# When the projections of the next heads must be finished: at the head boundary, or one unit ahead of it

## Chip, cores and metric

One NeuronCore of one Trainium2 chip runs the whole kernel. The metric is the device time of one execution in microseconds (us). The profile shows one execution with its engines: TensorE (PE for the matmuls, PEld for its weight loads), VectorE (DVE), ScalarE (ACT), GpSimd (POOL) and SyncE (SP, which here only issues transfers).

## The reference, cut to what matters

Two layers of a transformer-like trunk work on 512 latent tokens and 256 context tokens, all 1024 wide. In each layer a normalised input `h` is projected once, and three token mixers run on the result; their outputs are gated, merged and projected, and a mixture of 16 experts follows. The two mixers that matter here are both attentions:

```
ka, va, kb, vb, qa, qb, u, v, gates = _split(h @ w_in[i], KV_SIZES + Q_SIZES)
ya = neighbourhood_attn(qa, ka, va, kac, vac, na_rpb[i])      # A: 8 heads of 64, window + context keys
s  = einsum('bqhcd,bkhcd->bhcqk', q, k) * (dh ** -0.5)        # B: 4 heads, two softmax maps each
p  = softmax(s);  a = p[:, :, 0] - lam * p[:, :, 1];  yb = a @ v
```

In layer 0 the context tokens are computed too; in layer 1 they only give keys and values. So there are six attention stages: A and B for the context in layer 0, A and B for the latents in layer 0, A and B for the latents in layer 1.

## The kernel before, in words

**Units.** A stage A works through four pairs of heads (`pr` 0 to 3), a stage B through four double heads (`hd` 0 to 3). For each pair or head it goes through blocks of 128 queries, `b` from 0 to `nb - 1`: `nb` is 4 for the latents and 2 for the context. One (pair, block) is a unit. A unit has scores (`S`, line 487, matmuls of Q against K into PSUM), a softmax on VectorE and ScalarE (`soft`), transposes of the probabilities (`T`), the product with the values (`PV`) and an output step (`post`). `pipeline` (line 489) writes the units out so that the scores of the next unit stand ahead of the transposes of this one:

```
for i, u in enumerate(units):
    nxt = units[i + 1] if i + 1 < len(units) else None
    if nxt is not None:
        pre(nxt)
        S(nxt)
    ...
    F.pump(); T(u); ...soft(nxt); F.pump(); ...post(prev); PV(u); F.pump()
```

**Filler.** So that TensorE has work while a softmax runs, every other projection of the layer stands in a queue `F` (class `Filler`, line 48) of generators, each cut into small steps of three to twenty-four matmuls. `F.pump()` emits a share of what is left: `left / pumps`, in the planner's own microseconds, with 12 x `nch` pumps planned for a stage (`nch` is the number of blocks, so three pumps per unit). `F.finish(name)` emits steps until the named item is complete, whatever the share. The planner books a projection of 128 columns of output for 512 tokens as 24 matmuls and 5.12, and one step of three matmuls as 0.64; for 256 tokens half of it.

**Queue.** For stage A `mix` (line 804) pushes the values `va`, then for `i` = 1, 2, 3 the projections of K and Q of pair `i` (`kqa i`) and two gate projections, and last K and Q for the first head of stage B. For stage B it pushes the merge of A's output, the values `vb`, then `kqb i` with two gates each, and the gMLP's v. In layer 1 K is projected for the context tokens too, so a pair costs 12.80 instead of 10.24.

**K and Q.** `g_qk` (line 410) splits a weight tile in two halves (lines 153 and 155), multiplies (line 322), splits K (lines 349, 350), and likewise Q (`split_q`, lines 358 and 359). The half of Q that has to stand on the other 64 partitions is copied by a transfer from SBUF to SBUF, issued on ScalarE's queue (line 361), one for each of the two heads of a pair. The scores need that copy.

**Before the first score of a unit** stands `pre(nxt)`, which the change touches. Weights are loaded by SP (line 147), the bias of a unit in stage A too (line 537). The order that is written is a priority: the framework's scheduler then sets the order on each engine, and an instruction that is written later can run earlier when what stands ahead of it isn't ready by the scheduler's reckoning. Side work, vector products for the modulation of later layers (line 259, with its own weight loads), is handed out at a fixed rate for each microsecond of filler.

Of the kernel before, what the change touches and what calls it, by code (L numbers as in the profile page):

```python
# [38 lines left out]
def fr(ap):  # L39
    return ap.bitcast(F32)  # L40
# [68 lines left out]
class Trunk:  # L109
# [404 lines left out]
    def neighbourhood(self, c, F):  # L514
        nc, t = self.nc, self.t
        l, n, lat = c.l, c.n, c.lat
        nb = n // P
# [5 lines left out]

        def pre(u):
            pr, b = u
            if b == 0:
                F.finish(("kqa", pr))

        def S(u):
            pr, b = u  # L530
            K, Q = c.KQ["a", pr]
            qs = slice(b * P, (b + 1) * P)
            ps = self.p2([P, 2, 512])[:, :, :W]
            bias = None
            if lat:
                bias = self.tl([P, 2, 256], F32, "w2")
                nc.sync.dma_start(bias, t["bias"][l, pr, b])
            for hh in range(2):
                if not lat:
                    self.scores(ps[:, hh, :], Q, hh, qs, K[hh])  # L540
                    continue
                if KSTART[b] is None:
                    k = K[hh][:, 0:768].rearrange("p (a c) -> p a c", c=384)[:, :, 0:128]
                else:
                    k = K[hh][:, KSTART[b]:KSTART[b] + 256]
                self.scores(ps[:, hh, 256:512], Q, hh, qs, K[hh][:, NLAT:768])
                self.scores(ps[:, hh, 0:256], Q, hh, qs, k)
            st[u] = [ps, bias]
# [57 lines left out]
        def post(u):  # L606
# [7 lines left out]
            else:  # L614
                self.split_ps(y[pr][:, 0, :], y[pr][:, 1, :], yps)

        self.pipeline(F, [(pr, b) for pr in range(4) for b in range(nb)], pre, S, soft, T, PV, post)
        return y

# [13 lines left out]
    def differential(self, c, F, y):  # L633
        nc, t = self.nc, self.t
        l, n, lat = c.l, c.n, c.lat
        nk = 768 if lat else NCTX
        nt = nk // P
        nb = n // P
        st = {}

        def pre(u):
            hd, b = u
            if b == 0:
                F.finish(("kqb", hd))

        def S(u):
            hd, b = u
            K, Q = c.KQ["b", hd]
            qs = slice(b * P, (b + 1) * P)
            pss = []  # L650
            for m in range(2):
                ps = self.p2([P, nk])
                if lat:
                    self.scores(ps[:, n:], Q, m, qs, K[m][:, n:])
                self.scores(ps[:, :n], Q, m, qs, K[m][:, :n])
                pss.append(ps)
            st[u] = pss

        def soft(u):
            pss = st[u]  # L660
            ex, sm, rc = [], [], []
            for m in range(2):
                nm = self.st()
                nc.vector.tensor_reduce(out=nm, in_=pss[m], axis=AX.X, op=ALU.max, negate=True)
                e = self.tl([P, nk], F32, "e")
                s1 = self.st()
                nc.scalar.activation(e, pss[m], AF.Exp, bias=nm, accum_out=s1)
                r1 = self.st()
                nc.vector.reciprocal(r1, s1)
                ex.append(e)  # L670
                sm.append(s1)
                rc.append(r1)
            rat = self.st()
            nc.vector.scalar_tensor_tensor(out=rat, in0=sm[0], scalar=self.neglam[:, l:l + 1], in1=rc[1],
                                           op0=ALU.mult, op1=ALU.mult)
            nc.vector.scalar_tensor_tensor(out=ex[0], in0=ex[1], scalar=rat, in1=ex[0], op0=ALU.mult, op1=ALU.add)
            st[u] = [ex[0], rc[0]]

        def T(u):
            ex, rc = st[u]  # L680
            pT = self.tl([P, nk], F32, "e")
            for g in range(0, nt, 3):
                w = min(3, nt - g)
                tps = self.p1([P, w * P])
                for j in range(w):
                    nc.tensor.transpose(tps[:, j * P:(j + 1) * P], ex[:, (g + j) * P:(g + j + 1) * P], self.ident)
                nc.scalar.copy(pT[:, g * P:(g + w) * P], tps)
            st[u] = [pT, rc]

        def PV(u):  # L690
            hd, b = u
            F.finish("vb")
            pT, rc = st[u]
            V = c.V["b"]
            ops = self.p1([P, P])
            for j in range(nt):
                nc.tensor.matmul(ops, lhsT=pT[:, j * P:(j + 1) * P], rhs=V[j][:, hd * P:(hd + 1) * P],
                                 start=(j == 0), stop=(j == nt - 1))
            on = self.tl([P, P], F32, "w2")
            ss = self.st()  # L700
            nc.scalar.activation(on, ops, AF.Square, scale=rc, accum_out=ss)
            r = self.rstd(ss, P)
            sc = self.st()
            nc.vector.tensor_mul(sc, r, rc)
            nc.vector.tensor_scalar_mul(on, ops, sc)
            st[u] = on

        def post(u):
            hd, b = u
            qs = slice(b * P, (b + 1) * P)  # L710
            F.finish("mergeA")
            if not y:
                y.extend(self.ytiles(n))
            ot = self.p1([P, P])
            nc.tensor.transpose(ot, st[u], self.ident)
            g = self.subg[:, l:l + 1]
            nc.scalar.activation(y[hd][:, 0, qs], ot, AF.Copy, scale=g)
            nc.vector.scalar_tensor_tensor(out=y[hd][:, 1, qs], in0=ot, scalar=g, in1=fr(y[hd][:, 0, qs]),
                                           op0=ALU.mult, op1=ALU.subtract)

        self.pipeline(F, [(hd, b) for hd in range(4) for b in range(nb)], pre, S, soft, T, PV, post)
        return y

# [967 lines left out]
```

## Time and profile before

| | us |
|---|---|
| median of 3 runs | 2731.29 (2729.12 to 2732.53) |
| the profiled execution's own time | 2727.76 |
| its span in the trace | 2726.0 |
| TensorE busy in the span | 2491.0 (91%) |
| VectorE, ScalarE busy | 1674.9 (61%), 1238.0 (45%) |
| TensorE idle before a score that waited for the copy of Q | 23.6, 14 times |

The span is the time from the first to the last instruction of the program in that execution. The granted clock is the share of TensorE's full clock that it was given. "Idle before" is the time in which an engine did nothing just ahead of an instruction, and the name behind the arrow is what ended that time.

### The profile page before, as it was taken

The numbers are of one execution on the slowest core, as the hardware profiler recorded it, in microseconds if no ns is written. First come the engines' busy times: TensorE is split into PE (matmuls) and PEld (weight loads), VectorE is DVE, ScalarE is ACT, GpSimd is POOL, SyncE is SP. The second block draws the span as 40 slices with busy tenths as digits, with TensorE's granted clock in tenths as the row PEclk, the third lists the DMA queues.
The fourth block names the chain that finished last, engine by engine and source line by source line (L and its number), as shares of the span: only waits on it lengthen the run. The fifth ranks groups of instructions, "written<-read, shape, count | busy, mean of one in ns | idle before, by whom it ended". The sixth has DMA issues, their size and how long they took to land.

```text
span 2726.0 us, 35390 instructions
## 1 busy us (share of the span) xinstructions
PE 2491.0 (91%) x12856; PEld 1744.1 (64%) x12856; DVE 1674.9 (61%) x2841; ACT 1238.0 (45%) x2251; POOL 220.3 (8%) x155
## 2 busy tenths in 40 slices
PE   7898989999999789999999899998999969888886
PEld 5788877777788656666666687787788833111111
DVE  7567766878696579999999855656765341100002
ACT  4456445435623378888888655534453220000000
POOL 0000000001000011122222100000000011000000
PEclk8999999999999889999999999999999979999999
DMA  7465554343247689999999353252223579999998
GB/s 278 156 229 173 204 186 128 113 143 107 84 157 258 244 284 379 372 372 371 375 374 377 111 167 118 72 163 62 85 78 118 207 301 399 402 403 403 402 403 338
DMA packets 189278, 653.81 MB, mean 240 GB/s; under 512 B 22096, under 2 KB 26576, under 8 KB 189104
## 3 DMA queue, kind: packets, MB, share of 16 engines
q1 hardware_dynamic: 175648, 612.68, 60.6%
q0 software_dynamic: 8464, 25.96, 3.7%
q10 hardware_dynamic: 4992, 12.92, 1.8%
q8 instruction: 101, 1.65, 0.2%
q14 instruction: 73, 0.60, 0.1%
HBM read 615.03 MB, written 25.95 MB: 235 GB/s over the span
## 4 chain that ended last, share of the span: by engine, by line
PE 58%; DMA 20%; DVE 14%; ACT 5%; issue 2%; POOL 1%; SPq 0%; POOLq 0%; ACTq 0%; DVEq 0%
PE p L322 23%; PE p L1241 16%; DMA h<-in_w_e 5%; PE p L462 5%; DVE w L155 4%; PE p L1072 3%; PE p L1402 3%; DMA y<-in_w_e 3%; DMA w<-in_w_e 2%; DMA q<-q 2%; PE p L487 2%; DMA raw<-in_w_e 2%; DMA e<-in_w_e 2%; PE p L602 1%; ACT w L153 1%
## 5 line engine op out<-in xcount | busy, mean ns | idle before, releaser
L322 PE MATMUL p<-h,w 128*128 128x512 f32 (+1 forms) x4416 | 915.6, 358 | 16.3 <-DVE w L155 4.5
L322 PEld LDWEIGHTS p<-h,w 128*128 128x128 f32 x4416 | 710.4, 191 | 137.5 <-issue 11.8
L155 DVE TENSOR_TENSOR w<-raw,w 128x1024 fp32r<-128x1024 f32 x289 | 351.0, 1222 | 236.5 <-ACT w L153 208.8
L153 ACT CAST w<-raw 128x1024 fp32r<-128x1024 f32 x289 | 302.7, 1052 | 390.1 <-PE p L322 164.5
L1241 PE MATMUL p<-w,k 128*96 128x512 f32 x1536 | 376.0, 400 | 12.4 <-DVE w L155 9.6
L1241 PEld LDWEIGHTS p<-w,k 128*96 128x96 f32 x1536 | 238.9, 163 | 119.8 <-DVE w L155 20.9
L155 DVE TENSOR_TENSOR w<-h,w 128x1024 fp32r<-128x1024 f32 x156 | 185.5, 1220 | 10.1 <-ACT w L153 6.7
L167 POOL TENSOR_TENSOR st<-st,mhalf 128x1 f32<-128x1 f32 x76 | 57.4, 755 | 1564.4 <-DVE st L165 1564.4
L1241 PE MATMUL p<-w,q 128*96 128x512 f32 x768 | 180.0, 393 | 0.2 <-ACT q L1255 0.2
L153 ACT CAST w<-h 128x1024 fp32r<-128x1024 f32 x156 | 161.6, 1049 | 31.4 <-PE p L1241 27.2
L462 PE MATMUL p<-y,w 128*128 128x512 f32 (+1 forms) x864 | 175.0, 358 | 0.4 <-ACT y L342 0.3
L259 DVE SCALAR_TENSOR_TENSOR w<-raw,raw 128x1024 bf16<-128x1024 f32 x128 | 155.9, 1221 | 23.6 <-DMA raw<-in_w_adaT 16.5
L462 PEld LDWEIGHTS p<-y,w 128*128 128x128 f32 x864 | 142.6, 188 | 27.5 <-ACT y L342 0.8
L1241 PEld LDWEIGHTS p<-w,q 128*96 128x96 f32 x768 | 123.8, 161 | 53.7 <-ACT q L1255 0.4
L1435 ACT COPY q<-p 128x256 f32<-128x256 f32 x32 | 10.3, 375 | 303.3 <-PE p L1415 303.3
L487 PE MATMUL p<-k,q 128*128 128x256 f32 (+1 forms) x576 | 110.0, 323 | 30.7 <-DMA q<-q 23.6
L1333 POOL DMA_INDIRECT x1a<-tg,idx x16 | 96.0, 5997 | 457.9 <-DVE w L1287 408.8
L1447 DVE TENSOR_TENSOR v<-v,p 128x512 f32<-128x512 f32 x16 | 11.0, 688 | 171.0 <-PE p L1402 159.8
L487 PEld LDWEIGHTS p<-k,q 128*128 128x128 f32 x576 | 84.3, 196 | 47.4 <-issue 15.2
L1402 PE MATMUL p<-h,k 128*64 128x512 f32 x356 | 91.8, 628 | 16.9 <-DMA h<-in_w_e 16.6
L1427 DVE TENSOR_TENSOR k<-p,modAlat 128x256 f32<-128x256 f32 x32 | 12.1, 419 | 139.4 <-PE p L1415 139.4
L1072 PE MATMUL p<-w,h 128*128 128x512 f32 x384 | 91.1, 395 | 1.1 <-DVE w L155 1.1
(336 smaller groups left out, 3196.9 us busy)
## 6 DMA issues: line engine op xcount, KB each, us to landing
h<-in_w_e SPq DMA_DIRECT2D x288, 512.0 KB, 7.4
raw<-in_w_in SPq DMA_DIRECT2D x164, 512.0 KB, 3.5
raw<-in_w_e SPq DMA_DIRECT2D x120, 512.0 KB, 8.0
e<-in_w_e SPq DMA_DIRECT2D x96, 512.0 KB, 7.2
y<-in_w_e SPq DMA_DIRECT2D x96, 512.0 KB, 7.8
m<-in_w_e SPq DMA_DIRECT2D x92, 512.0 KB, 7.8
raw<-in_w_adaT SPq DMA_DIRECT2D x80, 512.0 KB, 3.9
w<-in_w_e SPq DMA_DIRECT2D x60, 512.0 KB, 10.2
```

The costliest lines, as they stand in the source:

```text
L153: nc.scalar.copy(hi, fr(raw))
L155: nc.vector.tensor_sub(lo, fr(raw), fr(hi))
L167: nc.gpsimd.tensor_tensor(out=r, in0=v, in1=self.mhalf, op=ALU.pow)
L259: nc.vector.scalar_tensor_tensor(out=dump, in0=fr(raw), scalar=1.0, in1=self.cb[v], op0=ALU.mult, op1=ALU.mult, accum_out=self.mod[s, l][: ...
L322: nc.tensor.matmul(ps, lhsT=w[a][:, k * P:(k + 1) * P], rhs=h[k][:, b, :], start=(k == 0 and i == 0), stop=(k == KD - 1 and i == 2))
L462: nc.tensor.matmul(bps, lhsT=wb[a][:, (jj * 4 + k) * P:(jj * 4 + k + 1) * P], rhs=y[k][:, b, :], start=(k == 0 and i == 0), stop=(k == 3 a ...
L487: nc.tensor.matmul(ps, lhsT=Q[:, h, i, qs], rhs=k, start=(i == 0), stop=(i == 1))
L602: nc.tensor.matmul(ypsd[pr][64 * hh:64 * hh + 64, b * P:(b + 1) * P], lhsT=V[vi][:, head * 64:(head + 1) * 64], rhs=pT[hh][:, j * P:(j + 1 ...
L1072: nc.tensor.matmul(banks[i][hf], lhsT=c.mh[k][:, a, i * P:(i + 1) * P], rhs=w[b][:, hf * BW:(hf + 1) * BW], start=(k == 0 and p == 0), sto ...
L1241: nc.tensor.matmul(ps[:, hf * 512:(hf + 1) * 512], lhsT=xt[a][:, k, :M], rhs=w[b][:, hf * 512:(hf + 1) * 512], start=(k == 0 and i == 0), ...
L1333: nc.gpsimd.indirect_dma_start(out=dst[:, :], out_offset=bass.IndirectOffsetOnAxis(ap=self.idx[:M, e:e + 1], axis=0), in_=y, in_offset=Non ...
L1402: nc.tensor.matmul(ps[half(h), :], lhsT=xT[:, k, :], rhs=w[:, h * BW:(h + 1) * BW], start=(k == 0), stop=(k == KD - 1))
```

## The change

In both attention stages the demand for the next pair's K and Q moves. Before, it stands ahead of the first unit of that pair (`b == 0`). After, only the first pair is asked for there; the next pair is asked for ahead of the scores of the last block of the current pair (`b == nb - 1`). `finish` emits all that stands in the queue ahead of the named item as well, so `va`, `mergeA`, `vb` or gates come along when they are still in the queue. Nothing is added or taken away; only the place in the written order changes, and with it how much the later pumps have left to hand out.

```
         def pre(u):
             pr, b = u
-            if b == 0:
+            if b == 0 and pr == 0:
                 F.finish(("kqa", pr))
+            if b == nb - 1 and pr < 3:
+                F.finish(("kqa", pr + 1))
...
         def pre(u):
             hd, b = u
-            if b == 0:
+            if b == 0 and hd == 0:
                 F.finish(("kqb", hd))
+            if b == nb - 1 and hd < 3:
+                F.finish(("kqb", hd + 1))
```

## Rows read from the trace of the kernel before

**Rows 1.** The page's first lines: span; busy time, share, instructions.

```profile
span 2726.0 us, 35390 instructions
PE 2491.0 (91%) x12856; PEld 1744.1 (64%) x12856; DVE 1674.9 (61%) x2841; ACT 1238.0 (45%) x2251; POOL 220.3 (8%) x155
```

**Rows 2.** Windows, one per attention stage in order, first score to last.

```profile
core 0: us, PE busy (x) PEld busy (x) DVE busy (x) ACT busy (x) POOL busy (x), PEclk, DMA share, GB/s
52.00:141.00 89.00, 76.06 (x600) 69.61 (x600) 57.17 (x101) 44.86 (x106) 0.00 (x0) 0.96 0.55 184
141.00:220.00 79.00, 71.23 (x565) 68.60 (x564) 50.56 (x108) 44.35 (x103) 4.19 (x6) 0.96 0.63 214
346.00:495.00 149.00, 136.35 (x808) 106.66 (x809) 88.92 (x204) 77.59 (x208) 0.00 (x0) 0.98 0.44 145
495.00:730.00 235.00, 224.13 (x1183) 181.48 (x1182) 188.03 (x367) 113.41 (x244) 15.78 (x16) 0.99 0.36 118
1588.00:1752.00 164.00, 160.91 (x1020) 130.66 (x1019) 84.49 (x201) 84.08 (x232) 0.00 (x0) 1.00 0.37 118
1752.00:1996.00 244.00, 229.23 (x1266) 191.36 (x1265) 158.89 (x287) 109.65 (x237) 8.23 (x14) 0.98 0.30 95
```

**Rows 3.** One line's view: all scores (line 487), TensorE, what ended its idle time.

```profile
  DMA q<-q: 23.6, 14
```

**Rows 4.** Timeline, TensorE: waits for Q at later pairs; start, busy us, [idle before].

```profile
73.51 0.50 PE L487 MATMUL p<-k,q 128*128 128x256 f32 x2 [2.14 <-DMA q<-q]
...
175.18 0.80 PE L487 MATMUL p<-k,q 128*128 128x256 f32 x2 [2.68 <-DMA q<-q]
...
1879.80 1.62 PE L487 MATMUL p<-k,q 128*128 128x256 f32 x4 [4.38 <-DMA q<-q]
...
1926.75 0.93 PE L487 MATMUL p<-k,q 128*128 128x256 f32 x4 [1.10 <-DMA q<-q]
```

**Rows 5.** Timeline, TensorE: the three such waits at a stage's first pair.

```profile
346.59 1.22 PE L487 MATMUL p<-k,q 128*128 128x256 f32 x8 [0.85 <-DMA q<-q]
...
352.73 2.04 PE L487 MATMUL p<-k,q 128*128 128x256 f32 x8 [4.21 <-DMA q<-q]
...
1775.88 0.94 PE L487 MATMUL p<-k,q 128*128 128x256 f32 x4 [0.32 <-DMA q<-q]
```

**Rows 6.** DMA view, 1870 to 1881 us: issues, KB each, median us to landing.

```profile
raw<-in_w_in SPq DMA_DIRECT2D x3, 512.0 KB, 7.2
q<-q ACTq DMA_DIRECT2D x2, 256.0 KB, 8.4
```

**Rows 7.** One line's view: all copies of Q (line 361), issue to landing.

```profile
DMA to landing us min/median/max: 2.3/3.7/8.9
```

**Rows 8.** Windows behind two long waits; the column behind POOL is the granted clock.

```profile
175.20:178.00 2.80, 2.80 (x13) 2.80 (x14) 0.85 (x3) 0.56 (x2) 0.00 (x0) 0.50 1.04 313
1879.80:1884.00 4.20, 4.17 (x11) 2.97 (x11) 1.58 (x2) 1.70 (x2) 0.00 (x0) 0.50 0.16 47
```

**Rows 9.** Timeline, TensorE: projections (line 322) at the full and at the lower clock.

```profile
114.19 1.43 PE L322 MATMUL p<-h,w 128*128 128x256 f32 x11
...
175.77 4.04 PE L322 MATMUL p<-h,w 128*128 128x256 f32 x18
...
1881.21 1.48 PE L322 MATMUL p<-h,w 128*128 128x512 f32 x3
```

**Rows 10.** One line's view: scores (line 487), TensorE, 1770 to 2000 us.

```profile
  ACT e L667: 4.1, 4
```

**Rows 11.** Lines by form, TensorE, 330 to 520 us: busy, mean ns | idle before.

```profile
L322 PE MATMUL p<-h,w 128*128 128x512 f32 x456 | 120.1, 407 | 1.0 <-DVE w L155 1.0
```

**Rows 12.** Timeline, TensorE: waits for a softmax in a last pair (context A, latent A, B).

```profile
118.97 0.30 PE L588 MATMUL p<-ident,e 128*128 128x128 f32 x1 [2.89 <-DVE e L580]
...
494.25 1.00 PE L588 MATMUL p<-ident,e 128*128 128x128 f32 x7 [1.00 <-DVE e L580]
...
1967.05 1.19 PE L322 MATMUL p<-h,w 128*128 128x512 f32 x4 [1.63 <-DVE w L705]
```

## The prediction

> **What bounds the kernel now.** I read the page first: TensorE is busy for 2491.0 of 2726.0 us [rows 1], so what any reordering can win is a part of the 235 us in which it is idle. Then the windows by attention stage [rows 2], since only these stages change: idle times (length less PE busy) are 12.9, 7.8, 12.7, 10.9, 3.1 and 14.8 us, 62 in sum. VectorE is the next engine and in no stage near its limit (188 of 235 at most). So TensorE sets the time there, and the question is what its idle time waits for. The view of the score line answers part of it: 23.6 us, in 14 waits, end with the landing of the copy of Q [rows 3]. The timeline shows where. Three of the 14 stand at the first pair of a stage, 5.4 us together [rows 5]; the change doesn't touch them. The other eleven, 18.3 us, stand at later pairs; the largest are 4.38 in the latent stage B of layer 1 and 2.68 and 2.14 in the context's stages [rows 4]. TensorE executes in order, so everything behind the waiting score waits too, ready filler among it.
>
> The copies explain the lateness: they land 2.3 to 8.9 us after issue, median 3.7 [rows 7]. In the stretch of the 4.38 us wait two copies took 8.4 us, beside three weight loads of 7.2 [rows 6].
>
> **What the change moves.** No instruction comes or goes, so the cost is all in the order. I walked the planner's ledger (0.64 for three matmuls of 512 tokens, half for 256) through both versions. Latent stage A of layer 0 as the example: the plan is 4 x (5.12 + 0.8) + 4 x 10.24 + 6 x 5.12 = 95.4 over 48 pumps. `va` is complete in the first unit, with 73.3 left and 46 pumps, so a pump hands out 1.6 and a unit 4.8. Pair 1 is complete two units into pair 0, and pairs 2 and 3 are 0.64 and 1.28 short at their boundaries, which `finish` emits there. After the change it emits 3.84, 2.56 and 3.20, one unit earlier. The 18 boundaries together:
>
> Context A: 8.08, 0, 2.24. Context B: 23.52, 0, 0. Latent layer 0 A: 3.84, 2.56, 3.20; B: 1.92, 0, 1.28. Latent layer 1 A: 5.76, 2.56, 4.48; B: 5.12, 0, 0.64.
>
> Five demands find nothing left to do, but even there the queue runs ahead of where it was. Two are large: with two blocks a pair, the context's first demand falls before the second unit's scores, and drags `va`, or `mergeA` and `vb`, ahead of them.
>
> Term 1, waits for Q. The moved work lies ahead of one more unit's scores, transposes, product and three pumps; a latent unit takes some 149/16 = 9.3 us in stage A of layer 0 [rows 2], more than the largest wait of 4.38 [rows 4] and the slowest landing of 8.9 [rows 7]. A context unit takes 89/8 = 11 us in A, fillers included. Upper bound 18.3. Lower bound 0, since the scheduler may place the scores earlier too, behind the same copies. In stage A of layer 1 the ledger meets two boundaries only at the last moment, and yet the whole stage is idle for 3.1 us [rows 2], so being late in the written order is not the whole cause; but the largest wait stands where copies took 8.4 us [rows 6], and there a unit's lead is enough. I take 70%: 12.8.
>
> Term 2, the clock. Behind the waits of 2.68 and 4.38 us the granted clock stood at 0.50, the 1.2 GHz level [rows 8]. Eighteen projection matmuls took 4.04 us there; at the full clock eleven took 1.43 [rows 9], so 18 x (0.224 - 0.130) = 1.7 us were lost. In the other place three projections took 1.48 [rows 9] where 0.263 each is normal [rows 11], and four scores 1.62 where 0.93 is [rows 4]: 1.4. Together 3.1, nothing at the least. It goes with its waits: 70%, 2.2.
>
> Term 3, waits that follow. When Q is late, the scores of two units run back to back and the second pair must wait until the exponentials free PSUM: 4.1 us in latent B of layer 1 [rows 10]. Bounds 0 and 4.1; half, 2.0, because the double buffer still holds only one unit there.
>
> Term 4, thinner cover, against the change. What `finish` takes early is missing from the later pumps. At the start of the last pair the ledger has 1.9, 2.6, 2.6, 1.3, 3.2 and 2.0 less left in the six stages (latent A of layer 0: 15.0 instead of 17.6), 13.6 in sum. A matmul of 512 columns takes 120.1/456 = 0.263 us [rows 11] where the planner books 0.213, so this is 16.8 us of real work. The last pairs already have uncovered softmaxes: 2.89, 1.00 and 1.63 us [rows 12]. If all of the missing filler turned into idle time, it would cost 16.8. It costs nothing if work of the next stage (values, gates) moves up into the gaps, as the written order is only a priority. I take 40%, 6.7: the last pairs show gaps, but each of them only one or two.
>
> Term 5, the context's second unit. Its scores now stand behind 8 or 23.5 units of filler, and its softmax behind them. The nearest row is the 2.89 us for which TensorE waited on a softmax after late scores [rows 12]; once per context stage is 5.8 at the most, nothing at the least if the scheduler still slips these scores in when filler waits for weights. I take 1.5.
>
> At nothing: the weight loads of the moved projections pass the bias loads on SP and the copies pass nothing on ScalarE's queue; buffers of K and Q for the next pair come free with the scores of the pair before the current one, one unit or more ahead. In latent B of layer 0 two more pieces of side work fall into the stage; VectorE has 47 us idle there [rows 2], and without that cover they would lengthen it by their own duration.
>
> Sum: -12.8 - 2.2 - 2.0 + 6.7 + 1.5 = -8.8. The profiled execution would go from its own 2727.8 to 2719.0. That one lies 3.5 below the median of the runs, so I forecast 2731.3 - 8.8 = 2722.5. All gains and no cost: 2731.3 - 25.5 = 2706. All costs and no gain: 2731.3 + 22.6 = 2754.
>
> **Rivals.**
>
> *The waits move along.* The scheduler places scores as soon as it reckons Q to be there; the same early work brings its weight loads, and the copies land as late after their issue as before. For it: the copies of 8.4 us beside the weight loads [rows 6], and stages where a lead of nearly a unit did not prevent 4.38 [rows 4]. Against it: scores keep their place behind the current pair's transposes and products, which have the higher priority. With 30% of terms 1 to 3 (7.7) and the costs as above (8.2) it ends at 2731 to 2732. That five demands find nothing to do belongs here too. The Trainium skill bears on this ("DMA: Bandwidth & Descriptors", Issuing engines are not separate DMA queues): transfers of all issuing engines run on the same 16 DMA engines and interleave, so a copy on ScalarE's queue has no lane of its own. The trace agrees, with 8.4 us beside weight loads against the median of 3.7; by that rule alone the waits would stay and the time with them, at this rival's 2731 to 2732.
>
> *The last pairs run dry*, the case on the other side. The place is the last pair of each stage, the price is term 4. With 70% of it (11.8), all of term 5 (5.8) and only 30% of the gains (7.7) the time is 2741. At those gains it is slower by over 0.2% as soon as 13.2 of the 22.6 us of costs come due; at the gains that I expect all of the 22.6 would be needed. For it: the gaps of rows 12. Against it: latent A of layer 1 is idle for only 3.1 us of 164 [rows 2], at a share that falls just as much before its last pair.
>
> **How the numbers follow.** No change by measurement means within 0.2%, 5.5 us, so 2725.8 to 2736.8. The forecast, -8.8, with its neighbours (70% of the gains against 20 to 60% of the costs, 2719 to 2726): 0.51. The waits move along: 0.28. The last pairs run dry: 0.21. The same three numbers are the chances of faster, same and slower. The range reaches from 2709, nearly all gains at a small cost, to 2739, which takes in the second rival and the nearer part of the third and leaves out about 2 in 10; the likeliest case's own range is 2709 to 2726.
>
> **What would show it.** In the profile after, the idle time of scores that ends with the copy of Q falls from 23.6 to about 11 us, 5.4 of it at first pairs; it stays over 18 if the waits move along. The stretches behind 172 and 1875 us show no clock of 0.50. Idle time that ends with lines 580, 589, 687 or 705 grows in the last pairs by 5 to 8 us together; by 15 or more if they run dry. The sum of idle time over the six stages falls from 62 to about 55. The expert stages, which the change doesn't touch, keep their length within 2 us; if they don't, the forecast is wrong for a reason that is not in it.

## The result, and the profile after

The changed kernel takes 2692.76 us (median of 4 runs, 2692.08 to 2694.26), the kernel before 2731.39. The ratio is 0.9864, with a 95% interval of 0.9851 to 0.9878: 1.36% faster, 38.6 us by the medians. The forecast had the direction right and the size wrong by a factor of more than four: 8.8 us, with a range that ended at 2709.

The page's first lines of the kernel after, which answer to [rows 1]:

```profile
span 2690.3 us, 35357 instructions
PE 2479.9 (92%) x12856; PEld 1741.7 (65%) x12856; DVE 1673.8 (62%) x2841; ACT 1239.6 (46%) x2253; POOL 228.0 (8%) x155
```

The span is 35.7 us shorter. TensorE's idle time fell from 235.0 to 210.4, by 24.6, and its busy time by 11.1 with the same 12856 matmuls.

To see where, I cut both traces at the first score of each attention stage; a window then goes to the first score of the next stage. Windows of the kernel before (length, PE busy with its count, and so on; the granted clock stands behind POOL), then of the kernel after:

```profile
52.40:137.60 85.20, 72.34 (x570) 66.09 (x569) 53.77 (x94) 42.68 (x101) 0.00 (x0) 0.96 0.54 177
137.60:346.60 209.00, 194.23 (x1423) 181.29 (x1421) 149.43 (x278) 112.55 (x220) 9.46 (x14) 0.98 0.59 202
346.60:522.80 176.20, 163.74 (x964) 127.81 (x964) 111.40 (x247) 89.32 (x235) 0.00 (x0) 0.98 0.41 134
522.80:1588.90 1066.10, 1007.85 (x4774) 750.57 (x4772) 903.88 (x1307) 679.27 (x993) 146.91 (x69) 0.98 0.74 264
1588.90:1775.90 187.00, 183.60 (x1154) 148.99 (x1153) 105.57 (x238) 94.67 (x255) 0.00 (x0) 1.00 0.35 114
1775.90:2726.00 950.10, 828.92 (x3786) 444.42 (x3786) 312.73 (x597) 198.04 (x410) 61.19 (x64) 0.97 0.71 269
```

```profile
50.70:127.00 76.30, 70.30 (x570) 64.75 (x569) 55.09 (x96) 42.53 (x101) 0.00 (x0) 0.98 0.64 198
127.00:335.10 208.10, 195.19 (x1423) 182.11 (x1421) 147.67 (x276) 114.76 (x222) 7.89 (x14) 0.98 0.63 203
335.10:498.30 163.20, 157.48 (x961) 124.90 (x961) 115.78 (x255) 89.20 (x235) 0.00 (x0) 1.00 0.49 152
498.30:1573.30 1075.00, 1011.13 (x4776) 753.57 (x4776) 899.14 (x1299) 679.79 (x995) 156.88 (x69) 0.97 0.74 261
1573.30:1754.50 181.20, 179.32 (x1153) 148.11 (x1153) 106.31 (x239) 94.18 (x254) 0.00 (x0) 1.00 0.37 118
1754.50:2690.30 935.80, 827.73 (x3786) 444.51 (x3786) 311.82 (x595) 197.48 (x410) 60.55 (x64) 0.97 0.72 273
```

The matmul counts agree within three, so the same work is compared. Context A is 8.9 us shorter, context B with what follows it 0.9, latent A of layer 0 13.0, latent A of layer 1 5.8, latent B of layer 1 with what follows 14.3; the piece that begins with latent B of layer 0 is 8.9 longer. Three facts stand out. Latent A of layer 0 gains 13.0 us, though its waits for Q at later pairs, which the change could remove, were only 2.7. Its idle time fell from 12.5 to 5.7 and its busy time by 6.3 as well. Some 4 of the 13.0 need not come from the move in this stage: the kernels `b_only` and `ctx_only` below leave its order alone, and there it is 172.0 and 172.2 us long. The other 9 are still far more than 2.7. And one piece gives 9 back.

The waits say what the idle time was. TensorE's waits in latent A of layer 0, before, and then after (us in total, times, longest; line 588 of before is 590 of after, 602 is 604):

```profile
PE p L487 <- DMA q<-q: 7.7, 5, 4.2
PE p L588 <- DVE e L580: 2.8, 4, 1.0
PE p L602 <- ACT e L589: 1.9, 3, 1.0
```

```profile
PE p L487 <- DMA q<-q: 5.2, 4, 2.3
PE p L590 <- DVE e L582: 1.3, 1, 1.3
PE p L604 <- ACT e L591: 0.2, 1, 0.2
```

The transposes and products that waited for a softmax waited 4.7 us before and 1.5 after. I had expected these to grow. How a late score comes back as such a wait can be followed at one boundary of the kernel before, on three engines:

```profile
404.07 1.22 PE L487 MATMUL p<-k,q 128*128 128x256 f32 x8 [0.59 <-DMA q<-q]
404.85 0.69 DVE L557 TENSOR_REDUCE st<-p 128x2 f32<-128x512 f32 x1 [3.42 <-PE p L487]
406.10 0.51 ACT L572 ACTIVATE e<-e,st 128x256 f32<-128x256 f32 x1 [4.93 <-DVE st L563]
409.88 1.11 PE L588 MATMUL p<-ident,e 128*128 128x128 f32 x8 [1.00 <-DVE e L580]
```

The score waits for the copy of Q. VectorE, which reduces the scores, has stood idle for 3.42 us by then, and ScalarE, which takes the exponentials, for 4.93. The transposes of this softmax wait another 1.00 us, and that wait is booked to line 580. At this score, 0.59 us of TensorE's time are booked to the copy.

For the whole program the view of the score line, which answers to [rows 3], has:

```profile
  DMA q<-q: 14.2, 12
```

The expert stages kept their length within 2 us, as forecast: the first and the last start of the first expert product of layer 0 were 965.1 and 1526.7, and are 948.4 and 1510.4.

### The profile page after: what moved, and what is told of

Same layout as the page of the kernel before. It is cut to its first block, busy times and chain, and to the rows that moved or that the text cites. A ratio compares the mean times of both kernels' runs of the same rounds, so it can differ in the third digit from the quotient of the medians.

```text
span 2690.3 us, 35357 instructions
## 1 busy us (share of the span) xinstructions
PE 2479.9 (92%) x12856; PEld 1741.7 (65%) x12856; DVE 1673.8 (62%) x2841; ACT 1239.6 (46%) x2253; POOL 228.0 (8%) x155
## 4 chain that ended last, share of the span: by engine, by line
PE 56%; DMA 22%; DVE 14%; ACT 5%; issue 2%; POOL 1%; ACTq 0%; SPq 0%; POOLq 0%; DVEq 0%
PE p L322 22%; PE p L1245 16%; DMA h<-in_w_e 6%; PE p L462 5%; DVE w L155 4%; PE p L1076 3%; DMA y<-in_w_e 3%; PE p L1406 3%; DMA w<-in_w_e 2%; DMA raw<-in_w_in 2%; PE p L487 2%; DMA raw<-in_w_e 2%; DMA q<-q 2%; ACT w L153 2%; DMA e<-in_w_e 1%
## 5 line engine op out<-in xcount | busy, mean ns | idle before, releaser
L1245 PE MATMUL p<-w,k 128*96 128x512 f32 x1536 | 376.4, 401 | 12.5 <-DVE w L155 9.6
L1337 POOL DMA_INDIRECT x1a<-tg,idx x16 | 101.4, 6336 | 448.8 <-DVE w L1291 399.7
L487 PE MATMUL p<-k,q 128*128 128x256 f32 (+1 forms) x576 | 106.7, 314 | 21.9 <-DMA q<-q 14.2
```

Of the source, the lines that this page charges most:

```text
L487: nc.tensor.matmul(ps, lhsT=Q[:, h, i, qs], rhs=k, start=(i == 0), stop=(i == 1))
L1245: nc.tensor.matmul(ps[:, hf * 512:(hf + 1) * 512], lhsT=xt[a][:, k, :M], rhs=w[b][:, hf * 512:(hf + 1) * 512], start=(k == 0 and i == 0), ...
L1337: nc.gpsimd.indirect_dma_start(out=dst[:, :], out_offset=bass.IndirectOffsetOnAxis(ap=self.idx[:M, e:e + 1], axis=0), in_=y, in_offset=Non ...
```

## The experiments

Theory 1, formed on these traces: what costs time is that Q is late for the first scores of a pair, and this costs far more than the waits that are booked to the copy of Q, because scores that come late make the softmax late and the transposes behind it wait. Rival 1: the gain comes from filler that runs earlier and denser, whatever Q does. Rival 2: any other order moves the time by tens of us, by luck. All times below are medians; before is 2729.7 to 2729.9 in these comparisons, and a ratio is to the kernel before.

### The two halves of the diff, and the context alone

Stages A alone, `a_only`: the first hunk of the diff without the second.

> The demand is moved in the three stages A alone; stages B keep the old place. Theory 1 (late Q: the scores of a new pair stand at the head of TensorE's queue until the copy of Q has landed, and the lateness comes back as softmax waits a few units later): the stages A keep what the work-aligned traces showed for them, about 9 in the context, 13 and 6 us in the two latent stages, so 2731 - 28 = 2703, at 2697 to 2710. Rival 2 (schedule luck: any other order of these stages moves the time by tens of us either way): no relation to those 28 us; anything from 2690 to 2745.

Stages B alone, `b_only`: the second hunk without the first.

> The demand is moved in the three stages B alone. Theory 1: the stage B of layer 1 gains about 13 us (its wait of 4.38 and what follows it), the one of layer 0 loses some 9, the context's gains 1: 2731 - 5 = 2726, at 2717 to 2733. With the A-only kernel the two differences add up to that of the full change, -38, within 6 us. Rival 2 (schedule luck): they don't add up.

The context alone, `ctx_only`: both hunks, used only where the stage is a context stage.

```
-            if b == 0:
+            ahead = not lat
+            if b == 0 and (pr == 0 or not ahead):
                 F.finish(("kqa", pr))
+            if ahead and b == nb - 1 and pr < 3:
+                F.finish(("kqa", pr + 1))
```

(The same in stage B.)

> The demand is moved in the two context stages alone. Theory 1, by the work-aligned traces: 11 us faster, 2716 to 2724. Term 5 as predicted (the context's second unit comes late) would take back what the waits give: within 6 us of before.

Measured: 2701.5 (ratio 0.9903, 0.9875 to 0.9930), 2716.5 (0.9952, 0.9934 to 0.9971) and 2714.6 (0.9953, 0.9935 to 0.9970). A and B give 1.0% and 0.5%; their sum of 1.45% agrees with the 1.36% of both, so rival 2 isn't needed for the size of the gain. It isn't gone for single pieces: as said above, latent A of layer 0 differs by 4 us between kernels that write it in the same order. The context alone gives 15 us by the medians, over a third of the gain, at a place where term 5 had a cost. B alone gained more than I had expected (13 instead of 5), because I had counted 9 us of loss in latent B of layer 0 as the work of the moved demand. Most of that is not: the piece is nearly as long where no demand is moved in it or in the stage ahead of it. In `ctx_only`:

```profile
505.90:1579.30 1073.40, 1014.00 (x4773) 755.84 (x4771) 903.78 (x1308) 680.10 (x994) 151.13 (x69) 0.97 0.73 262
```

That is 1073.4 us against 1066.1 in the kernel before and 1075.0 in the changed one. With A alone it is 1073.2, with B alone 1071.8. The trace of the kernel before is the exception here, and why is open.

### The copy of Q without a transfer

The order stays as it was, and GpSimd makes the copy; once in the order of before, once in the changed one:

```
-            nc.scalar.dma_start(fr(Q[other, h]), fr(Q[own, h]))
+            nc.gpsimd.tensor_copy(Q[other, h], fr(Q[own, h]))
```

> The order of before, but the copy of Q to the other partitions is made by GpSimd instead of a transfer; the demand for K and Q stays at the head boundary. Theory 1 (late Q): scores no longer wait for a landing, so most of the gain comes without moving any demand: 2700 to 2712. Rival 1 (the gain is from filler that runs earlier and denser, not from Q): the time stays within 8 us of before, 2723 to 2735, since no filler is moved.

> The order of the changed kernel, and the copy of Q made by GpSimd. Theory 1: the 14.2 us of waits for the copy that are left go as well, but the big ones are gone: 2675 to 2690. The difference to the order of before with the same copy shrinks to under 15 us, as both were about the same lateness. Rival 1: the change is worth as much as with the transfer, 30 to 40 us between these two.

Measured: 2675.3 in the order of before (0.9815, 0.9786 to 0.9845) and 2678.5 in the changed one (0.9819, 0.9793 to 0.9846). This decides between theory 1 and rival 1. (The first of the two is faster than the 2700 to 2712 that I had expected.) With a faster copy and no demand moved, the old order is faster than the changed kernel; and on top of the faster copy the change is worth nothing. One line's view of the copy on GpSimd, in the old order (min/median/max ns):

```profile
L361 POOL CAST q<-q x48: 606/1039/2098, 46.1 to 1914.5; 64x1024 fp32r<-64x1024 f32 x32, 64x512 fp32r<-64x512 f32 x16
```

It takes 1.0 us in the median, where the transfer landed after 3.7 [rows 7]. The page of that kernel:

```profile
span 2673.8 us, 35388 instructions
PE 2467.7 (92%) x12856; PEld 1733.4 (65%) x12856; DVE 1678.5 (63%) x2841; ACT 1237.9 (46%) x2251; POOL 280.3 (10%) x203
```

Idle time is 206.1, 28.9 less than before, while the waits that are booked to the copy fell only from 23.6 to 12.0:

```profile
  POOL q L361: 12.0, 15
```

So 17 of the 29 us of idle time were booked to something else. TensorE's busy time fell too, by 23.3 us. The granted clock has a part in that; its means over the span, before, with the order changed, and with GpSimd's copy in the order of before:

```profile
core 0: 2726.0 us, clock 0.973
core 0: 2690.3 us, clock 0.973
core 0: 2673.8 us, clock 0.978
```

An estimate from these numbers: 2726.0 x 0.027 = 74 us were lost to the lower clock before and 2673.8 x 0.022 = 59 with GpSimd's copy, so at most some 15 of the 52 us between the two spans are the clock. Between the two orders it makes about 1 us in these executions. TensorE's waits in latent A of layer 0 with GpSimd's copy, in the order of before, all of them:

```profile
PE p L462 <- DVE w L628: 0.6, 1, 0.6
```

The softmax waits of that stage are gone, with the written order and the filler of before. So thin cover alone does not explain them; the chain of rows above shows late scores as their cause at one boundary.

To rule out that it is GpSimd as an engine that helps, the same copy is written by ScalarE and VectorE, which are the busier ones:

```
-            nc.scalar.dma_start(fr(Q[other, h]), fr(Q[own, h]))
+                nc.scalar.copy(Q[other, h, 0, d:d + w], fr(hi))
+                nc.vector.tensor_copy(Q[other, h, 1, d:d + w], fr(Q[own, h, 1, d:d + w]))
```

> The order of before; the halves of Q for the other 64 partitions are written by ScalarE and VectorE themselves, which takes four to eight more short instructions a pair on each and no transfer. Theory 1: no landing to wait for, so like GpSimd's copy, 2672 to 2700. If it were GpSimd that mattered (an engine of its own, not the missing transfer), the additional work on VectorE and ScalarE, about 1.5 us a pair on each, would take most of the gain back: 2710 to 2735.

Measured: 2674.7 (0.9784, 0.9756 to 0.9813), the same as with GpSimd. So it is not GpSimd; what the two have in common is that there is no transfer whose landing has to be awaited. They also take the 48 issues off ScalarE's queue, where the kernel before has:

```profile
L361 ACTq DMA_DIRECT2D q<-q x48: 467/468/517, 46.1 to 1964.5; - x48
```

That is some 22 us of ScalarE's queue in all, and the exponentials run there too. The same transfer issued from another queue was not run, so how the gain divides between the landing and the issue is not shown. At the boundary in the rows above the exponentials did not stand behind an issue: ScalarE was idle. And the moved order, which keeps every issue, gains 38.6 us by itself. Both versions, in the old order, beat the changed kernel by 17 to 18 us and the one before by 54 to 55.

### Which boundaries

GpSimd copies only at the 18 boundaries that the change moves, `pool_later`, or only at the first pair of each stage, `pool_first` (the condition is turned round); the order is that of before:

```
+            if not first:
+                nc.gpsimd.tensor_copy(Q[other, h], fr(Q[own, h]))
+            else:
+                nc.scalar.dma_start(fr(Q[other, h]), fr(Q[own, h]))
```

> The order of before; GpSimd makes the copy of Q for the later pairs and heads (the 18 boundaries that the change moves), the first of each stage keeps its transfer. Theory 1: the change's gain without its order: 2688 to 2702. If a large part of the gain came from elsewhere than these boundaries, 2705 to 2725.

> The order of before; GpSimd makes the copy of Q for the first pair or head of each of the six stages alone, which the change doesn't touch. Theory 1: the rest of the 54 us that GpSimd's copy gains in all, 10 to 20 us faster: 2710 to 2720. If the gain of the change is a matter of luck at other places, about as much as at the later ones.

Measured: 2681.6 (0.9821, 0.9807 to 0.9835) and 2724.8 (0.9981, 0.9972 to 0.9990). At the moved boundaries the copy without a transfer is worth 48 us, at the first pairs 5. Both were outside what I had expected, the split being still more one-sided. That the 5 us are about what is booked to the waits of the first pairs (5.4 us, [rows 5]) fits a reading in which no softmax is in flight there that a late score could hold up. It may also be chance: in that trace latent A of layer 0 is 7.0 us shorter than before and the piece behind it 5.7 longer.

### Thinner cover by itself

About twice what the change takes from the last pairs (31.2 of the planner's units against 13.6), in the order of before and with no demand moved; ahead of the scores of the last pair's first unit, `thin`, and behind them, `thin_behind`:

```
             if b == 0:
                 F.finish(("kqa", pr))
+            if b == 0 and pr == 3:
+                F.run(5.2)
...
             st[u] = [ps, bias]
+            if b == 0 and pr == 3:
+                F.run(5.2)
```

(The first addition is `thin`, the second `thin_behind`; the same in stage B.)

> The order of before, with 5.2 planner units of filler forced ahead of the scores at the start of the last pair of every stage, twice what the change took from there; no demand moves. It is the thinner cover of term 4 by itself (K and Q of the next stage's first head come a little earlier too). Term 4 as predicted: 6 stages x 5.2 x 1.23 = 38 us of cover less, at 40% 15 us slower, 2740 to 2750. Theory 1 with a cover that doesn't matter: within 6 us of before.

> The order of before, with 5.2 planner units of filler forced in the last pair of each stage behind the scores of its first unit (the kernel with the thinner cover forced it ahead of them and so made these scores late too). Term 4 alone, if thin cover costs: 2738 to 2750 again. If the 15 us of the earlier kernel came from the late scores: within 6 us of before, 2724 to 2736.

Measured: 2747.1 (1.0055, 1.0035 to 1.0075) and 2744.6 (1.0053, 1.0037 to 1.0070), 15 to 17 us slower. The place makes no difference, so it is not the delay of these scores; thinner cover does cost. The 15 us are about 40% of the 38 us of work that was taken away, as term 4 had it, but that may overstate the price: with `thin_behind`, 10 of the 18 us between the two spans stand in the piece from latent B of layer 0 on, and that piece is longer than before by some 5 us or more in kernels with untouched cover too. The waits of the whole program in `thin_behind`, first those of before, then its own (line 715 of before is 719, 588 is 590):

```profile
PE p L588 <- DVE e L580: 7.1, 8, 2.9
PE p L715 <- DVE st L744: 2.6, 1, 2.6
PE p L715 <- DVE w L705: 2.0, 4, 1.3
```

```profile
PE p L590 <- DVE e L582: 9.7, 7, 6.1
PE p L719 <- DVE w L709: 4.4, 6, 1.7
PE p L719 <- DVE st L748: 4.2, 1, 4.2
```

### The copy made twice

Two equal transfers one behind the other, in the order of before and in the changed one:

```
             nc.scalar.dma_start(fr(Q[other, h]), fr(Q[own, h]))
+            nc.scalar.dma_start(fr(Q[other, h]), fr(Q[own, h]))
```

> The order of before, with each copy of Q made twice by two equal transfers one behind the other, so that it lands later. Theory 1: each of the 24 copies lands 1 to 3 us later and the scores wait for both, so 20 to 50 us slower: 2750 to 2780. Rival 1 (the copy is not what counts): within 6 us of before; the transfers take 12 MB more, which is 2% of the kernel's traffic.

> The changed kernel with each copy of Q made twice. Theory 1: the lead of a unit covers part of the later landing, so it loses less than the order of before does with the same doubling: 2700 to 2725, and the distance between the two orders grows from 38 to 45 us or more. Rival 1: the distance stays at 38.

Measured: 2846.6 (1.0429, 1.0404 to 1.0454) and 2753.2 (1.0080, 1.0056 to 1.0104). The distance between the orders grows from 38 to 93 us, which is the way theory 1 has it. Both are far slower than I had expected (2750 to 2780, and 2700 to 2725), and the size is not clean: in the first of them each of the 48 second transfers is issued only when the one ahead of it has landed, and it waits for that on ScalarE's queue, where the exponentials stand behind it. At one place:

```profile
494.88 0.47 ACTq L361 DMA_DIRECT2D q<-q  x1
...
498.23 0.47 ACTq L362 DMA_DIRECT2D q<-q  x1
498.74 0.61 ACTq L361 DMA_DIRECT2D q<-q  x1
502.53 0.47 ACTq L362 DMA_DIRECT2D q<-q  x1
```

### Two units of lead, and half a copy

Two units ahead, `two_ahead`:

```
-            if b == nb - 1 and pr < 3:
+            if b == max(nb - 2, 0) and pr < 3:
```

> The demand for the next pair two units ahead (where a pair has only two blocks, ahead of its first unit's successor as before in the changed kernel, or at its own first unit), instead of one. Theory 1: with one unit of lead 14.2 us of waits for the copy are left; a second unit removes some of them but thins the cover more, so near the changed kernel, 2685 to 2703. If lead alone were the cause the time would go on to the 2675 of the order with GpSimd's copy.

Measured: 2692.2 (0.9853, 0.9823 to 0.9882), equal to one unit. Asking for K and Q two units ahead gains nothing over one.

Half a copy, in both orders:

```
-            nc.scalar.dma_start(fr(Q[other, h]), fr(Q[own, h]))
+            nc.scalar.dma_start(fr(Q[other, h, 0]), fr(Q[own, h, 0]))
...
-            nc.tensor.matmul(ps, lhsT=Q[:, h, i, qs], rhs=k, start=(i == 0), stop=(i == 1))
+        nc.tensor.matmul(ps, lhsT=Q[:, h, 0, qs], rhs=k, start=True, stop=False)
+        nc.tensor.matmul(ps, lhsT=Q[own, h, 1, qs], rhs=k[own], start=False, stop=True)
```

> The order of before, with half the copy: only the high half of Q goes to the other 64 partitions, and the second matmul of a score, with the low half of Q, contracts over 64 partitions alone. It leaves out the products of the low half of Q with the low half of K. Theory 1: a copy of half the bytes lands earlier by some 1 us, and as doubling cost 117 us, halving gains a good part of what GpSimd's copy gains: 2690 to 2715. Rival 1 (the copy's landing doesn't matter, only where the filler stands): 2723 to 2735.

> The changed kernel with half the copy, in the same way (the products of the low halves are left out). Theory 1: 2675 to 2692, and the distance between the two orders shrinks from 38 to under 25 us. Rival 1: the distance stays at 38.

Measured: 2793.4 (1.0215, 1.0180 to 1.0249) and 2766.0 (1.0125, 1.0095 to 1.0155), slower where I had expected faster. It shows little of the copy, because the scores themselves became expensive. Lines by form in latent A of layer 0, in the order of before; first with half the copy, then the scores of the kernel before:

```profile
L488 PE MATMUL p<-k,q 64*128 64x256 f32 x66 | 26.3, 398 | 0.0
L487 PE MATMUL p<-k,q 128*128 128x256 f32 x66 | 24.8, 375 | 3.0 <-DMA q<-q 3.0
```

```profile
L487 PE MATMUL p<-k,q 128*128 128x256 f32 x128 | 20.5, 299 | 8.0 <-DMA q<-q 7.7 <-ACT e L569 0.3
```

The scores of about one stage take 51.1 us there instead of 20.5. The distance between the orders did shrink, from 38 to 27, which is the way theory 1 has it, but with such a difference in the scores themselves it proves little.

## Why the prediction was right and wrong, step by step

**What bounds the kernel**: right in the main. The gain lies in the attention stages, and 24.6 of the 35.7 us are idle time of TensorE. But I had said that a reordering can only win idle time, and 11.1 us came from TensorE's busy time.

**Term 1**, waits for Q at later pairs: right in kind, and too optimistic in its share. The waits booked to the copy fell from 23.6 to 14.2 us, where the forecast said about 11; 5.5 of the 14.2 stand at first pairs, as forecast. The later pairs went from 18.3 to 8.7, so 9.6 us came instead of 12.8. My list of the largest waits before had left one out, 2.64 us in context A (the sum of 18.3 has it):

```profile
113.61 0.74 PE L487 MATMUL p<-k,q 128*128 128x256 f32 x4 [2.64 <-DMA q<-q]
```

The two longest at later pairs that are left:

```profile
102.99 0.60 PE L487 MATMUL p<-k,q 128*128 128x256 f32 x2 [1.83 <-DMA q<-q]
...
1934.66 0.94 PE L487 MATMUL p<-k,q 128*128 128x256 f32 x4 [2.27 <-DMA q<-q]
```

**Term 2**, the clock: right for its two places; its size was not measured by itself. The two stretches of [rows 8] have their full clock again, but the lower clock comes in other places: the piece from latent B of layer 0 on is granted 0.97 instead of 0.98, and the mean over the span is 0.973 in both kernels. Windows of the kernel after around the work of [rows 8]:

```profile
167.00:181.00 14.00, 12.68 (x105) 11.98 (x104) 11.40 (x29) 10.68 (x30) 1.09 (x2) 1.00 0.69 218
1830.00:1880.00 50.00, 48.00 (x272) 40.34 (x271) 39.35 (x75) 25.51 (x54) 3.10 (x4) 1.00 0.20 64
```

**Term 3**, waits that follow: this is the step that failed. "When Q is late, the scores of two units run back to back and the second pair must wait": I counted that for one stage, 4.1 us, took half, and set 25.5 us as the upper bound of all gains. A copy without a transfer at the moved boundaries is worth 48 us, where 18.3 us of TensorE's waits were booked to Q. The change itself won 38.6 us, while the waits booked to Q at these boundaries fell by 9.6. The rest sits in waits for a softmax a few units behind the boundary and in TensorE's shorter busy time (11.1 us less after, 23.3 less with GpSimd's copy, of which the clock can be up to 15); how it divides was not measured. The bound should not have been the sum of the waits with the copy's name on them: the same late score stands behind the waits of lines 588 and 602, which I had filed under something else.

**Term 4**, thinner cover: right that it costs, wrong in evidence. The two thin kernels cost 15 us for 38 us of cover, 40%, so the change's own 16.8 would cost about 6.7, the forecast's own figure, or less. But the "already uncovered softmaxes" [rows 12] that I took for proof of a thin cover came with late Q: in latent A of layer 0 they vanish with a faster copy at unchanged cover. The waits that end with lines 580, 589, 687 or 705 should have grown by 5 to 8 us in the last pairs; in latent A of layer 0 they fell from 4.7 to 1.5 for the whole stage. So I booked the same rows as a cost of the change when they were part of its gain. What the change wins, 38.6, is some 10 less than the 48 of a copy without a transfer; 8.7 us of waits for Q that are left and the price of term 4 can account for that, but this split was not measured.

**Term 5**, the context's second unit: no net loss to be seen. The context alone gains 15 us by the medians, and context B with what follows it is not longer. A small loss inside these gains isn't excluded.

**The rivals.** The waits did not move along: they would have stayed over 18 us, and 14.2 are left. The copies themselves land no earlier after their issue than before (2.2 to 6.6 us, median 4.3, against 2.3 to 8.9 and 3.7); what changed is where the scores stand behind them. The rule that the prediction named from the Trainium skill ("DMA: Bandwidth & Descriptors", Issuing engines are not separate DMA queues) is about the transfers, and these landing times say nothing against it; the step from there to waits that stay was the wrong one. The last pairs did not run dry, though thin cover has a price: that rival went with gains of only 7.7 us, and the change won 38.6 net of all costs.

**Left open**: why the piece from latent B of layer 0 on is some 5 us or more shorter in the kernel before than in every other kernel here, what TensorE's shorter busy time consists of beyond the clock, how the gain of a copy without a transfer divides between its landing and its issue on ScalarE, and how far the scheduler's other placements of single instructions contribute within a stage.

## What to carry to other kernels

When a late operand holds up an in-order engine at the head of a software pipeline, the waits with that operand's name can be far less than what it costs (here 18.3 us against 48): look for waits on the later steps of the same pipeline a few units behind each late one, and count them too before calling them lack of cover. Prove it by making the operand early in another way, as a faster copy does here, before tuning the order around it: once the copy was fast, the order no longer mattered. In this kernel a small copy between partitions on the critical chain was better made by engines than by a transfer, whether GpSimd made it or ScalarE and VectorE together.

## What I had not expected of the hardware

A copy of 64 x 1024 or 64 x 512 values to the other 64 partitions took GpSimd 1.0 us in the median (0.6 to 2.1), and replacing 48 transfers by it saved 54 us. Score matmuls that contract over 64 partitions, alternating with those over 128 into the same accumulation, kept TensorE busy for 0.40 us each (26.3 us for 66), and those over 128 between them for 0.38, where the stage's scores of 256 columns took 0.16 each before (20.5 us for 128).
